# Moving layout transfers to GpSimd and one half of the early recurrences into the projection, in a hybrid gMLP, DeltaNet and attention block

## The chip, the cores and the metric

One core of one Trainium2 chip. The metric is the device time of one execution in microseconds; lower is better. TensorE is called PE below (PEld is its weight load), VectorE DVE, ScalarE ACT, GpSimd POOL and SyncE SP.

## The reference

One sequence of 1024 positions with 2048 channels, in float32. What is computed:

```python
h = rmsnorm(x, ln_g)
proj = h @ w_in
(g_u, g_v, g_z, d_q, d_k, d_v, d_z, d_a, d_b, c_q, c_z) = jnp.split(proj, SPLIT_POINTS, axis=-1)
out_a = gmlp_spatial_gating(g_u, g_v, ...) * silu(g_z)            # 4 groups of 128
q, k, v = split(causal_conv_silu(concat([d_q, d_k, d_v]), conv_w))  # 8 heads of 128
q, k = l2norm(q) * 128 ** -0.5, l2norm(k)
o = gated_delta_rule(q, k, v, g, beta)                           # chunks, state carried along the sequence
out_b = rmsnorm(o, dn_norm_g) * silu(d_z)
out_c = attention(c_q, rmsnorm(mem) @ w_mem_kv) * silu(c_z)      # 256 memory tokens, 4 heads of 128
y = rmsnorm(x + concat([out_a, out_b, out_c]) @ w_out, final_g)
```

In the gated delta rule every chunk needs the inverse of a unit lower triangular matrix `a + eye`, with `a` made from k, beta and the decays; after that a state of 128 x 128 for each head is carried from chunk to chunk.

## The kernel before

The sequence is worked on in two halves of 512 positions (`hf` 0 and 1). Every large product is done as three products of float32r parts: a value is split into `hi` (a cast on ACT, `split_to`) and `lo` (a subtraction on DVE).

The order in which the program is written is not the order in which it is issued. Each call (`S` is ACT, `V` DVE, `G` POOL, `PE` TensorE, `Q` SP) goes to `Plan.add`, which records what it reads and writes. `Plan.price` gives every operation an estimated cost, and for a transfer the time until it has landed. `Plan.issue` then plays the program through with these estimates, on each engine always taking the ready operation of the lowest rank (`rank(...)`, 5 where nothing is said; matmuls of the projection have 9), and issues the operations in the order of their estimated starts. From then on each engine keeps its order: an operation that has to wait holds back all that stand behind it on its engine. Nearly all transfers are issued by SP (`Q.dma_start`).

The stages, in the order of the program:

- Keys and values of the memory, and the normalised rows of x in transposed form (`ahi`, `alo` hold the first half; the second half goes to DRAM as `hTd`).
- The early projection, for heads 0 to 3 alone (pairs p = 0 and 1): `project` computes a column of 128 channels from weight pieces of 4 x 128 rows (four buffers `wraw`). `front(p, hf)` does q and k of a pair: `conv`, then `qk` with the decay mask (POOL's `affine_select` on `E`), the matrices of the chunks into `gt`, and everything stored to DRAM (`late_d`, `gt_d`). `early_values` does v. All this first for half 0; then `refill` loads half 1 into `ahi` and `alo`, and it is done again.
- `blocks_out` writes the diagonal 32 x 32 blocks of `gt` to DRAM (`gdr`, four transfers for a pair and half). `inverse` gathers them into one tile with a block on each partition (`G.dma_start`, `inv<-gdr`), inverts all of them with 62 instructions on DVE, and stores the inverses and their transposes (`tdr`, `udr`). For the early heads it runs once, with the four `gdr` of both halves, on 128 partitions, at rank 3. It uses the two buffers of `inv`, which `qk` needs too.
- The rest of the input projection, five column blocks (`blocks(0)` to `blocks(4)`), each by seven products for two halves of x and two column groups (`seven`), with sums of operands made before (`left_sums`).
- The recurrences. For a pair and half `front_late` loads what was stored, `levels` gathers the inverted blocks (`blocks_in`) and composes the full inverse `ut`, and `back` runs four scan steps and writes the heads' output. For heads 0 to 3 they are written ahead of `blocks(0)` at rank 2.6, and run beside it:

```python
    def backs(ps, inv):
        for hf in range(2):
            for p in ps:
                state = front_late(p, hf, inv[hf * 2 + p % 2])
                ut = levels(state[2], *state[-1])
                if p >= NJ // 2:
                    values(*state)
                back(*state, ut)
```

- Heads 4 to 7 (pairs 2 and 3): their fronts after `blocks(0)`, their inverse ("late") after `blocks(1)`, their recurrences after `blocks(2)`.
- The output projection, seven products for each of two column pairs, and the final norm.

Of the kernel before, what the change touches and what calls it, by code (L numbers as in the profile page):

```python
# [44 lines left out]


class Op:
    __slots__ = ("eng", "fn", "args", "kw", "cls", "idx", "cost", "lat", "nbytes", "lock", "n", "succ", "ready", "at",
                 "lead", "tail", "table")


# [9 lines left out]
class Plan:  # L61
    SEEN = {"pe": 55.0, "act": 35.0, "dve": 35.0, "pool": 78.0, "sp": 60.0}
    SLACK = 600.0
    OVERLAP = {"pe": 0.0, "act": 90.0, "dve": 80.0, "pool": 50.0, "sp": 0.0}
    DMA_RATE = 300.0
    DMA_FIXED = 1600.0
    SWITCH = 250.0
    TABLES = {AF.Exp: "exp", AF.Silu: "silu", AF.Gelu_apprx_tanh: "gelu"}
    TABLE_LOAD = 1500.0
# [113 lines left out]
    def price(self, o, name, outs, ins):  # L183

        out = outs[0]
        n = math.prod(out.shape[1:])
        both = [*outs, *ins]
        psum = any(i.space == PSUM for i in both)
        pointer = any(i.shape[-1] == 1 and math.prod(i.shape[1:]) == 1 for i in ins[1:])
        o.nbytes = o.lock = 0  # L190
        o.lat = 0.0
        if name == "dma_start":
            o.cost = {"sp": 380.0, "act": 430.0, "pool": 1000.0}[o.eng]
            rows = math.prod(out.shape[:-1])
            o.nbytes = max(4 * math.prod(out.shape), 512 * rows)
            src = ins[0]
            pieces = src.shape[-1] < 128 or out.shape[-1] < 128
            if out.space == DRAM:
                o.lat = 9000.0 if out.shape == (32, 8, 32) else 3000.0
            elif pieces or out.shape[0] < 32:  # L200
                o.lat = 2400.0
            elif list(src.ap)[0][0] == 0:
                o.lat = 4000.0
        elif o.eng == "pe":
            passes = 1 if ins[0].dtype == F32R else 2 if name == "transpose" else 4
            o.cost = max(13.3 + n / 2.4 * passes, 222.0 if passes == 4 else 110.0) if out.shape[0] == P else 30.0
            o.lat = 175.0
        elif o.eng == "act":
            o.cost = (165.0 if psum else 200.0) + 0.82 * n + (105.0 if pointer else 0.0)
            o.cost += 190.0 if "accum_out" in o.kw else 0.0  # L210
        elif o.eng == "dve":
            n = max([n] + [math.prod(i.shape[1:]) for i in ins])
            o.cost = (n + 151) / 0.96 + (60.0 if pointer and name == "scalar_tensor_tensor" else 0.0)
            o.lock = not psum and (name.startswith("tensor_") or name == "scalar_tensor_tensor")
            o.lock = o.lock and name != "tensor_reduce"
        else:
            o.lock = 1
            if name in ("memset", "affine_select"):
                o.cost = 100.0 + 0.83 * n * (1 if name == "memset" else 1.4)
                o.lat = 800.0 if name == "affine_select" else 0.0  # L220
            else:
                o.cost = 750.0 + 150.0 * (n - 1) if n < 8 else 200.0 + 2.1 * n

    def issue(self):
# [10 lines left out]
        while left:  # L235
# [22 lines left out]
            for o in (head, *head.tail):  # L258
                t = max(t, free[e])
                if o.table not in (None, table):  # L260
                    t, table = t + self.TABLE_LOAD, o.table
                o.at = t
                left -= 1
                if o.lock:
                    t = max(t, held["pool" if e == "dve" else "dve"])
                end = t + o.cost
                if o.lock:
                    held[e] = end
                free[e] = end - min(self.OVERLAP[e], 0.5 * o.cost)
                done = end + o.lat  # L270
                if o.nbytes and e == "act":
                    beside = max(beside, end) + 2 * o.nbytes / self.DMA_RATE
                    done = beside + self.DMA_FIXED + o.lat
                elif o.nbytes:
                    dma = max(dma, end) + o.nbytes / self.DMA_RATE
                    done = dma + self.DMA_FIXED + o.lat
                for s in o.succ:
                    if s.eng != e or o.nbytes:
# [17 lines left out]
def kernel(  # L296
# [35 lines left out]
    def DT(shape, name, dt=F32):  # L332
        return dr.tile(list(shape), dt, name=name, tag=name)[:]
# [382 lines left out]
    NJ = NH // 2  # L716
# [241 lines left out]
    def blocks_out(gt, n):  # L958

        gv = gt.rearrange("p h t i -> p (h t) i")  # L960
        gdr = [DT([8, 32, 32], f"gdr{n}_{b}") for b in range(4)]
        for b in range(4):
            sl = slice(b * 32, (b + 1) * 32)
            with rank(1):
                S.dma_start(gdr[b].rearrange("c j i -> j c i"), gv[sl, :, sl])
        return gdr

    def flat(start, *aps):
# [2 lines left out]
    def inverse(gdrs, n, cls):  # L971
# [13 lines left out]
        with rank(cls):  # L985
# [240 lines left out]
    def halves(t):  # L1226
# [208 lines left out]
        project_pair(c, lambda hf, b, t, y: dones[b](hf, t, y), dest)  # L1435


    def backs(ps, inv):
        for hf in range(2):
            for p in ps:  # L1440
                state = front_late(p, hf, inv[hf * 2 + p % 2])
                ut = levels(state[2], *state[-1])
                if p >= NJ // 2:
                    values(*state)
                back(*state, ut)
# [93 lines left out]


    with rank(2.6):
        backs(range(NJ // 2, NJ), late_inv)


    def both(c, j, hf, t, y):
# [226 lines left out]
```

## Time and profile before

| | us |
|---|---|
| median of 3 runs | 1661.45 |
| lowest and highest run | 1657.06, 1662.36 |
| the profiled execution, its own time | 1662.46 |
| its span, from first to last instruction | 1660.7 |
| mean granted clock of TensorE | 0.992 |

The profile's times count from the start of the span. "L292" is the line in `Plan.issue` through which every operation is issued, so groups are told apart by the tiles that they write and read: `out<-in`, with the numbers of buffers left out. ACTq, POOLq and SPq are those engines' instruction queues, where transfers are issued. In a list of waits stand the time in total, how often, and the longest; in an order of time the start, the length, the instruction, its count, and in brackets the idle time ahead of it and what ended it. In a list of transfers stand the count, the KB of each and the median time from issue to landing.

### The profile page before, as it was taken

How to read it: one execution, taken by the hardware profiler on the slowest of the kernel's cores; microseconds unless marked ns; L12 is line 12 of the kernel's file. 1: busy time of each engine (PE TensorE's matmuls, PEld its weight loads, DVE VectorE, ACT ScalarE, POOL GpSimd, SP SyncE). 2: the span in 40 equal slices, each digit the busy share in tenths (PEclk: the TensorE clock that was granted, in tenths of full speed). 3: DMA queues.
4: the chain of work that ended last, by engine and by line, in shares of the span. 5: the costliest groups of instructions: out<-in, count | busy, mean ns of one | idle time of the engine just before them, and what ended most of it. 6: DMA issues, size and time to landing. Idle time of an engine off the chain costs nothing.

```text
span 1660.7 us, 26037 instructions
## 1 busy us (share of the span) xinstructions
PE 1623.1 (98%) x8570; PEld 1357.9 (82%) x8570; DVE 1253.7 (75%) x2081; ACT 1027.4 (62%) x2226; POOL 109.2 (7%) x166
## 2 busy tenths in 40 slices
PE   8999999999899999999999998999999999999997
PEld 7888888887788888878887886888888878788886
DVE  4865777778666567989998885777768887688875
ACT  5957765765275556987775345776666774345445
POOL 0000100130000000100013000000000000000001
PEclk9999999999999999999999999999999999999999
DMA  7887888797888886599878977788968769679746
GB/s 253 241 235 222 256 288 244 231 311 269 280 270 263 283 273 201 192 283 337 294 250 274 303 230 205 232 263 305 312 209 291 264 220 353 202 251 307 227 140 241
DMA packets 320625, 427.88 MB, mean 258 GB/s; under 512 B 58669, under 2 KB 139238, under 8 KB 320490
## 3 DMA queue, kind: packets, MB, share of 16 engines
q1 hardware_dynamic: 308290, 418.87, 77.6%
q10 hardware_dynamic: 10088, 4.21, 1.0%
q0 software_dynamic: 2112, 3.15, 0.7%
q8 instruction: 67, 1.10, 0.3%
q14 instruction: 68, 0.56, 0.1%
HBM read 338.52 MB, written 87.06 MB: 256 GB/s over the span
## 4 chain that ended last, share of the span: by engine, by line
PE 82%; DMA 7%; DVE 5%; ACT 2%; issue 2%; SPq 0%; ACTq 0%; DVEq 0%; POOLq 0%; POOL 0%
PE acc L292 62%; PE dn L292 21%; DMA wraw<-in_w_in_dram 2%; DVE wlo L292 1%; DMA wraw<-hTd 1%; DMA wraw<-in_w_out_dram 1%; DVE alo L292 1%; ACT whi L292 1%; DMA y<-in_w_in_dram 1%; DVE y L292 0%; SPq L292 0%; ACTq L292 0%; DMA hTd<-tn 0%; ACT ahi L292 0%; DVE wraw L292 0%
## 5 line engine op out<-in xcount | busy, mean ns | idle before, releaser
L292 PE MATMUL acc<-ahi,whi 128*128 128x512 f32 (+1 forms) x1152 | 451.0, 392 | 1.2 <-ACT whi L292 0.9
L292 PE MATMUL acc<-alo,whi 128*128 128x512 f32 (+1 forms) x1152 | 451.0, 392 | 0.0
L292 PE MATMUL acc<-ahi,wlo 128*128 128x512 f32 (+1 forms) x1152 | 450.3, 391 | 0.2 <-DVE wlo L292 0.2
L292 PEld LDWEIGHTS acc<-ahi,whi 128*128 128x128 f32 x1152 | 217.3, 189 | 43.4 <-ACT whi L292 1.3
L292 PEld LDWEIGHTS acc<-ahi,wlo 128*128 128x128 f32 x1152 | 217.2, 189 | 41.5 <-DVE wlo L292 0.8
L292 PEld LDWEIGHTS acc<-alo,whi 128*128 128x128 f32 x1152 | 217.1, 188 | 40.7
L292 PE MATMUL acc<-ahi,zh 128*128 128x512 f32 x736 | 237.1, 399 | 6.0 <-DVE y L292 5.0
L292 DVE TENSOR_TENSOR wlo<-wraw,whi 128x512 fp32r<-128x512 f32 (+1 forms) x170 | 157.3, 926 | 73.9 <-ACT whi L292 64.5
L292 ACT CAST whi<-wraw 128x512 fp32r<-128x512 f32 (+1 forms) x170 | 137.3, 808 | 121.8 <-PE acc L292 69.1
L292 DVE TENSOR_TENSOR alo<-raws,ahi 128x1024 fp32r<-128x1024 f32 x131 | 159.7, 1220 | 51.0 <-ACT ahi L292 48.3
L292 ACT CAST ahi<-raws 128x1024 fp32r<-128x1024 f32 x131 | 137.4, 1049 | 62.2 <-PE dn L292 28.2
L292 PEld LDWEIGHTS acc<-ahi,zh 128*128 128x128 f32 x736 | 138.7, 191 | 33.9 <-ACT whi L292 5.4
L292 PE MATMUL acc<-ahi,zl 128*128 128x512 f32 x368 | 146.3, 397 | 0.0
L292 DVE TENSOR_TENSOR ahi<-y,ahi 128x1024 fp32r<-128x1024 f32 x65 | 79.2, 1218 | 34.6 <-ACT ahi L292 24.2
L292 ACT CAST ahi<-y 128x1024 fp32r<-128x1024 f32 x65 | 68.1, 1048 | 45.2 <-PE acc L292 20.3
L292 PEld LDWEIGHTS acc<-ahi,zl 128*128 128x128 f32 x368 | 70.1, 190 | 13.7
L292 ACT CAST zh<-wraw 128x1024 fp32r<-128x1024 f32 x36 | 37.8, 1050 | 42.2 <-PE acc L292 25.2
L292 DVE TENSOR_TENSOR zl<-wraw,zh 128x1024 fp32r<-128x1024 f32 x36 | 43.9, 1220 | 21.5 <-ACT zh L292 21.3
L292 PE MATMUL dn<-wlo,ahi 128*128 128x512 f32 x152 | 59.0, 389 | 0.0
L292 PE MATMUL dn<-whi,alo 128*128 128x512 f32 x152 | 59.0, 389 | 0.0
L292 PE MATMUL dn<-whi,ahi 128*128 128x512 f32 x152 | 58.8, 389 | 0.0
L292 POOL TENSOR_TENSOR small<-small,mhalf 128x1 f32<-128x1 f32 x26 | 17.1, 662 | 627.7 <-DVE small L292 627.7
(387 smaller groups left out, 3105.0 us busy)
## 6 DMA issues: line engine op xcount, KB each, us to landing
wraw<-in_w_in_dram SPq DMA_DIRECT2D x268, 256.0 KB, 4.4
raws<-sd SPq DMA_DIRECT2D x148, 256.0 KB, 4.0
y<-in_w_in_dram SPq DMA_DIRECT2D x92, 256.0 KB, 4.7
y<-sd SPq DMA_DIRECT2D x77, 256.0 KB, 4.7
wraw<-in_w_out_dram SPq DMA_DIRECT2D x64, 256.0 KB, 4.1
raws<-h0d SPq DMA_DIRECT2D x54, 256.0 KB, 5.1
y<-in_w_out_dram SPq DMA_DIRECT2D x33, 256.0 KB, 4.1
sd<-zg SPq DMA_DIRECT2D x32, 256.0 KB, 5.9
```

What stands on the lines that cost most here:

```text
L292: o.fn(*o.args, **o.kw)
```

## The change

It does four things.

- The transfers of `blocks_out` (32 in all) go from ACT's queue to POOL's. So do the stores of `inverse`, which become two for each inverse (`tdr`, `udr` over all its partitions) in place of two for each 32 partitions.
- The estimates in `Plan.price` for transfers: the time on the transfer engines is computed from packets (8.5 ns and 0.0368 ns for each byte of a packet, over 16 queues) in place of 300 bytes for each ns; the fixed part is 2900 in place of 1600 ns; issue costs and additional latencies are changed.
- The early inverse is done in two: "early0" with the two `gdr` of half 0, written after the values of half 0, and "early1" with those of half 1, both at rank 5.5.
- The recurrences of pairs 0 and 1 in half 0 are written (rank 2.6) into the projection of half 1, each after the front of the same pair in half 1. Those of half 1 stay ahead of `blocks(0)`. The clearing of the `ut` buffers is written earlier, and `early_values` of half 1 takes PSUM bank 2 or 3 of `dn` for its transposes in place of an `acc` bank.

```diff
@@ class Plan
-    DMA_RATE = 300.0
-    DMA_FIXED = 1600.0
+    PACKET = (8.5, 0.0368)
+    QUEUES = 16
+    DMA_FIXED = 2900.0
@@ def price
-            o.cost = {"sp": 380.0, "act": 430.0, "pool": 1000.0}[o.eng]
-            rows = math.prod(out.shape[:-1])
-            o.nbytes = max(4 * math.prod(out.shape), 512 * rows)
+            o.cost = {"sp": 440.0, "act": 430.0, "pool": 700.0}[o.eng]
             src = ins[0]
-            pieces = src.shape[-1] < 128 or out.shape[-1] < 128
+            run = 4 * min(out.shape[-1], src.shape[-1])
+            fixed, byte = self.PACKET
+            o.moves = 4 * math.prod(out.shape) / run * (fixed + byte * run) / self.QUEUES
             if out.space == DRAM:
-                o.lat = 9000.0 if out.shape == (32, 8, 32) else 3000.0
-            elif pieces or out.shape[0] < 32:
-                o.lat = 2400.0
+                o.lat = 3000.0 if run < 512 else 1500.0
             elif list(src.ap)[0][0] == 0:
-                o.lat = 4000.0
+                o.lat = 3500.0
@@ def issue
-                elif o.nbytes:
-                    dma = max(dma, end) + o.nbytes / self.DMA_RATE
+                elif o.moves:
+                    dma = max(dma, end) + o.moves
                     done = dma + self.DMA_FIXED + o.lat
...
@@ def blocks_out
-                S.dma_start(gdr[b].rearrange("c j i -> j c i"), gv[sl, :, sl])
+                G.dma_start(gdr[b].rearrange("c j i -> j c i"), gv[sl, :, sl])
@@ def inverse
-        tdr, udr = ([DT([32, 32, 32], f"{t}{n}_{i}") for i in range(len(gdrs))] for t in ("tdr", "udr"))
-        for i in range(len(gdrs)):
-            with rank(1):
-                flat(S.dma_start, tdr[i], ti[i * 32 : (i + 1) * 32])
-                flat(S.dma_start, udr[i], gd[i * 32 : (i + 1) * 32])
-        return list(zip(tdr, udr))
+        tdr, udr = (DT([nr, 32, 32], f"{t}{n}") for t in ("tdr", "udr"))
+        with rank(1):
+            flat(G.dma_start, tdr, ti)
+            flat(G.dma_start, udr, gd)
+        return [(tdr[i : i + 32], udr[i : i + 32]) for i in range(0, nr, 32)]
@@ def early_values
-        by_token(vs, to_tokens((v, tpb()))[0], late_hs[:, hf, h, 1])
+        by_token(vs, to_tokens((v, work() if hf else tpb()))[0], late_hs[:, hf, h, 1])
@@ the early projection
     for h in range(NJ):
         early_values(h, 0)
+    with rank(2.6):
+        early_inv = inverse(gdrs, "early0", 5.5)
+
+    def one_back(p, hf, inv):
+        state = front_late(p, hf, inv)
+        ut = levels(state[2], *inv)
+        if p >= NJ // 2:
+            values(*state)
+        back(*state, ut)
...
     first = project([column(0, 0), column(1, 0)], before)
     decays(1, a)
-    gdrs += [front(0, 1, first), front(1, 1)]
-    with rank(3):
-        early_inv = inverse(gdrs, "early", 3)
+    for u in ring["ut"].bufs:
+        G.memset(u, 0.0)
+    gdrs = []
+    for p in range(2):
+        gdrs.append(front(p, 1, first if p == 0 else (None, None)))
+        with rank(2.6):
+            one_back(p, 0, early_inv[p])
+    with rank(2.6):
+        early_inv = inverse(gdrs, "early1", 5.5)
     for h in range(NJ):
         early_values(h, 1)
-    for u in ring["ut"].bufs:
-        G.memset(u, 0.0)
@@ ahead of blocks(0)
     with rank(2.6):
-        backs(range(NJ // 2), early_inv)
+        for p in range(NJ // 2):
+            one_back(p, 1, early_inv[p])
     blocks(0, to_conv(0), to_conv(1))
@@ after blocks(2)
     with rank(2.6):
-        backs(range(NJ // 2, NJ), late_inv)
+        for n, inv in enumerate(late_inv):
+            one_back(NJ // 2 + n % 2, n // 2, inv)
```

More of the change, by code (lines that the diff above doesn't have):

```diff
@@ L47 @@
 class Op:
-    __slots__ = ("eng", "fn", "args", "kw", "cls", "idx", "cost", "lat", "nbytes", "lock", "n", "succ", "ready", "at",
+    __slots__ = ("eng", "fn", "args", "kw", "cls", "idx", "cost", "lat", "moves", "lock", "n", "succ", "ready", "at",
                  "lead", "tail", "table")
@@ L189, in price @@
         pointer = any(i.shape[-1] == 1 and math.prod(i.shape[1:]) == 1 for i in ins[1:])
-        o.nbytes = o.lock = 0
+        o.moves = o.lock = 0
         o.lat = 0.0
         if name == "dma_start":
-            o.cost = {"sp": 380.0, "act": 430.0, "pool": 1000.0}[o.eng]
-            rows = math.prod(out.shape[:-1])
-            o.nbytes = max(4 * math.prod(out.shape), 512 * rows)
+            o.cost = {"sp": 440.0, "act": 430.0, "pool": 700.0}[o.eng]
             src = ins[0]
-            pieces = src.shape[-1] < 128 or out.shape[-1] < 128
+            run = 4 * min(out.shape[-1], src.shape[-1])
+            fixed, byte = self.PACKET
+            o.moves = 4 * math.prod(out.shape) / run * (fixed + byte * run) / self.QUEUES
             if out.space == DRAM:
-                o.lat = 9000.0 if out.shape == (32, 8, 32) else 3000.0
-            elif pieces or out.shape[0] < 32:
-                o.lat = 2400.0
+                o.lat = 3000.0 if run < 512 else 1500.0
             elif list(src.ap)[0][0] == 0:
-                o.lat = 4000.0
+                o.lat = 3500.0
         elif o.eng == "pe":
@@ L270, in issue @@
                 done = end + o.lat
-                if o.nbytes and e == "act":
-                    beside = max(beside, end) + 2 * o.nbytes / self.DMA_RATE
+                if o.moves and e == "act":
+                    beside = max(beside, end) + 2 * o.moves
                     done = beside + self.DMA_FIXED + o.lat
-                elif o.nbytes:
-                    dma = max(dma, end) + o.nbytes / self.DMA_RATE
+                elif o.moves:
+                    dma = max(dma, end) + o.moves
                     done = dma + self.DMA_FIXED + o.lat
                 for s in o.succ:
-                    if s.eng != e or o.nbytes:
+                    if s.eng != e or o.moves:
                         when = done + self.SEEN[s.eng] + (self.SLACK if s.eng == "pe" else 0.0)
@@ L1435, in blocks @@
         project_pair(c, lambda hf, b, t, y: dones[b](hf, t, y), dest)
[L1438 to L1445, printed above, removed]
     with rank(2.6):
-        backs(range(NJ // 2), early_inv)
+        for p in range(NJ // 2):
+            one_back(p, 1, early_inv[p])
     blocks(0, to_conv(0), to_conv(1))
```

## The prediction

> **What bounds the kernel now.** I read the page first, then a table of busy time by stage, then the waits of TensorE (PE), then ScalarE's (ACT's) instructions around the two worst stages.
>
> ```profile
> PE 1623.1 (98%) x8570; PEld 1357.9 (82%) x8570; DVE 1253.7 (75%) x2081; ACT 1027.4 (62%) x2226; POOL 109.2 (7%) x166
> ```
> ```profile
> 0.00:100.00 100.00, 91.28 (x543) 78.48 (x543) 62.69 (x106) 68.19 (x135) 6.37 (x18) 0.97 0.83 256
> 100.00:430.00 330.00, 327.64 (x1570) 271.43 (x1571) 248.57 (x504) 213.53 (x570) 30.85 (x45) 1.00 0.83 260
> 430.00:450.00 20.00, 15.04 (x55) 11.88 (x54) 11.27 (x15) 5.04 (x5) 0.00 (x0) 0.83 0.68 208
> 450.00:1000.00 550.00, 546.18 (x2992) 458.24 (x2991) 435.36 (x714) 356.15 (x763) 53.57 (x74) 1.00 0.81 267
> 1000.00:1020.00 20.00, 13.16 (x110) 10.21 (x110) 13.94 (x20) 8.93 (x15) 1.34 (x3) 0.83 0.75 195
> 1020.00:1630.00 610.00, 607.41 (x3229) 509.41 (x3218) 463.95 (x690) 356.86 (x706) 12.25 (x18) 1.00 0.76 251
> 1630.00:1661.00 31.00, 22.36 (x99) 18.20 (x97) 17.94 (x34) 18.73 (x34) 4.81 (x8) 0.91 0.74 271
> ```
>
> The columns of the table: the stretch, its length, busy time of PE, weight loads, DVE, ACT and POOL (in us), granted clock, DMA share, GB/s. PE nearly always has work, so an edit pays only where it removes idle time or slow clock of PE. Away from the beginning and the end there are two such places. 430 to 450 has 4.96 us of idle and, at clock 0.83, 20 x 0.17 = 3.4 us of lost clock: 8.4 us. 1000 to 1020 has 6.84 and 3.4: 10.2 us. The three long stages between them leave 2.36 + 3.82 + 2.59 = 8.8 us idle together.
>
> ```profile
> PE dn L292 <- DVE el L292: 6.8, 1, 6.8
> PE acc L292 <- DVE y L292: 5.0, 1, 5.0
> ```
> ```profile
> 425.95 1.71 ACTq L292 DMA_DIRECT2D tdrearly<-inv  x3
> 428.78 5.05 ACTq L292 DMA_DIRECT2D udrearly<-inv  x3
> 435.37 0.31 ACTq L292 DMA_DIRECT2D tdrearly<-inv  x1
> 436.09 0.31 ACTq L292 DMA_DIRECT2D udrearly<-inv  x1
> 436.50 1.04 ACT L292 CAST ahi<-y 128x1024 fp32r<-128x1024 f32 x1 [10.15 <-DMA udrearly<-inv]
> ```
> ```profile
> 437.57 1.22 DVE L292 TENSOR_TENSOR ahi<-y,ahi 128x1024 fp32r<-128x1024 f32 x1 [7.56 <-ACT ahi L292]
> ```
> ```profile
> 989.05 3.73 ACTq L292 DMA_DIRECT2D tdrlate<-inv  x4
> 995.51 6.34 ACTq L292 DMA_DIRECT2D udrlate<-inv  x4
> 1001.95 0.62 ACT L292 CAST whi<-kT 128x512 fp32r<-128x512 f32 x1 [12.15 <-DMA tblk<-tdrlate]
> ```
>
> The waits show one wait of PE for each place, both put down to DVE. ACT's order of time shows what stood behind DVE: the eight stores of an inverse (tdr, udr) sit in ACT's own queue, drawn out over 10 and 12 us although a single issue takes 0.31, and the casts of the next operands stand behind them. `ahi` comes 10.15 us late, DVE waits 7.56 for it, and PE runs dry. At 989 it happens again with `whi`.
>
> **The change, part by part.** *The stores of the inverses leave ACT.* Two GpSimd (POOL) transfers for each of three inverses replace sixteen on ACT, so the casts wait for nothing but their data. I count both places as gone: 8.4 + 10.2 = 18.6 us. That is also the most that can be had there. From below: where a load or DVE's own work is next, part of each stays; half is the value I take for that case, 9.3.
>
> *The 32 transfers out of `gt` leave ACT too.*
>
> ```profile
> L292 ACTq DMA_DIRECT2D gdr<-gt x32: 309/469/2578, 187.2 to 888.9; - x32
> gdr<-gt ACTq DMA_DIRECT2D x32, 32.0 KB, 5.1
> inv<-gdr POOLq DMA_DIRECT2D x32, 32.0 KB, 5.4
> L292 POOL DMA_DIRECT2D inv<-gdr x32 | 16.9, 533 | 39.1 <-DMA raws<-sd 18.1 <-DVE hs L292 16.4 <-DMA inv<-gdr 3.3
> L292 POOL DMA_DIRECT2D gt<-kvd x2 | 1.5, 745 | 13.2 <-issue 13.2
> ```
>
> ACT loses 32 x 0.469 = 15 us of issue; PE waits for none of it in the list above, so I count nothing. POOL gets 32 + 6 issues at 0.53 to 0.75 us, 20 to 28 us on an engine busy for 109. Landing is about the same in the rows (5.4 against 5.1). Behind a POOL transfer that waits for an inverse stand the mask of the next head's decay (`affine_select` on E), the rsqrt of `hs` and the clears of `ut` and `gt`; ACT's exponential waits for the mask, and weight casts stand behind that. Between nothing and the 10 to 12 us that ACT lost; I take nothing, since POOL is idle in nine tenths of its time.
>
> The Trainium skill speaks against this part: SBUF — State Buffer, section "SBUF: two separate sides", says that a DMA issued from GpSimd can't write its descriptors while DVE runs a two-port operation such as an fp32 copy within SBUF, with an issue of 620 ns becoming 3100. By that figure the 38 issues would hold POOL for 38 x 3.1 = 118 us, an estimate, and rival 2 below would be the likeliest. The trace does not bear it out for this mix of DVE work: the 32 issues average 533 ns.
>
> *One inverse becomes two.* DVE pays by elements per partition; half as many heads only halve the partitions.
>
> ```profile
> 377.00:427.00 50.00, 0.00 (x0) 0.00 (x0) 22.20 (x63) 0.00 (x0) 0.00 (x0) 1.00 0.83 285
> 298.85 0.64 POOL L292 TENSOR_SCALAR_AFFINE_SELECT E<-E 128x512 f32<-128x512 f32 x1 [83.10 <-ACT vs L292]
> ```
>
> The first row is the time of the instructions on `inv` alone: 63 of DVE, 22.2 us. So DVE gets 22.2 us more. The second row shows the room: POOL has been idle for 83.1 us, since the last `hs` of the first half's heads, when the first mask of the second half comes at 298.85, and in between nobody wants the two `inv` buffers. Should the inverse, at the low rank 5.5, last beyond 299, the second half's heads wait for `inv`, and PE still has the other columns to project.
>
> *The first half's recurrences of two pairs move from the block after into the projection.*
>
> ```profile
> 230.00:300.00 70.00, 69.77 (x324) 57.16 (x323) 51.38 (x103) 40.20 (x95) 0.64 (x1) 1.00 0.83 254
> 300.00:380.00 80.00, 79.95 (x386) 66.75 (x385) 58.19 (x123) 55.81 (x172) 18.43 (x26) 1.00 0.92 282
> 380.00:430.00 50.00, 49.09 (x220) 40.15 (x219) 48.02 (x88) 24.70 (x35) 0.20 (x2) 1.00 0.85 294
> 460.00:660.00 200.00, 198.92 (x1285) 169.89 (x1285) 131.47 (x204) 122.86 (x290) 11.31 (x18) 1.00 0.78 255
> ```
> ```profile
> 439.00:660.00 221.00, 28.84 (x176) 26.03 (x176) 8.59 (x28) 7.51 (x32) 0.98 0.78 251
> 439.00:660.00 221.00, 19.29 (x112) 17.04 (x112) 8.72 (x28) 0.00 (x0) 0.98 0.78 251
> 439.00:660.00 221.00, 4.40 (x32) 3.84 (x32) 8.59 (x28) 32.04 (x130) 0.98 0.78 251
> ```
> ```profile
> L292 SPq DMA_DIRECT2D kT<-late x8: 320/348/454, 337.7 to 597.6; - x8
> ```
> ```profile
> kT<-late SPq DMA_DIRECT2D x16, 256.0 KB, 4.3
> gt<-gtd SPq DMA_DIRECT2D x8, 512.0 KB, 4.8
> ```
> ```profile
> 1521.80 43.52 PE acc L292 x192
> ```
>
> PE's work only changes its place: 0. The three rows of 439 to 660 are the instructions on `steps`, `states` and `vs` while four recurrences ran: DVE (8.59 + 8.72) / 4 = 4.3 us for one, ACT (7.51 + 32.04) / 4 = 9.9, and some 4 of copies in `levels`. From 230 to 380 DVE has 18.6 + 21.8 = 40.4 us free and gets 22.2 + 2 x 4.3 = 30.8; ACT has 54.0 free and gets 28. Both fit. DMA is tighter. A recurrence loads ten tiles of 256 KB and one of 512, gathers the inverse's blocks (0.3 MB) and stores two tiles, 4.0 MB in all, which at 282 / 0.92 = 307 GB/s fills the engines for 13 us. Two are 26, of which the first one's loads (3.1 MB, 10 us) run before 430 already (`kT<-late` begins at 337.7): 16 us more. Free are 11.9 + 6.4 + 7.5 = 25.8 us over the three rows. Each load is also one more place in SP's queue ahead of a weight load, at rank 2.6 against 4; four weight pieces are buffered, of 12 matmuls at 43.52 / 192 = 0.227 us each, so 10.9 us of cover against a burst of 10. Bounds: 0, and 16 + 10 - 6.4 = 19.6 us when all 26 falls on the fullest row, 300 to 380. I take 4 us, nearest to the last of the four rows, where recurrences ran at a DMA share of 0.78 and PE lost 1.1 us in 200, and more than that because this stage is fuller. What the following block gains by losing two of its four recurrences is at most that 1.1.
>
> *The new estimates* (a transfer's time by its packets, 2.9 us fixed for 1.6) reorder every queue. The rows above say loads land after 4 to 5 us, so the order should fit better; the 8.8 us of small idle time may shrink or double. I take 0.
>
> **Sum.** The profiled execution took 1662.5 us (span 1660.7), 1.0 above the median of 1661.45. 1662.5 - 18.6 + 4 = 1647.9, or 1647 against the median.
>
> **Rivals.** *1, slower: the projection starves.* The two bursts of loads and the second inverse fall where DMA is at 0.92 and DVE between 0.73 and 0.96. If all 19.6 us becomes idle time of PE, and the clock falls with it as at 1000 (10.2 lost for 6.84 idle, a factor 1.5), it costs 29: 1662.5 - 18.6 + 29 - 1 = 1672. It turns to a loss from 12.4 us of idle on. For it: no DMA row is as full as 300 to 380. Against it: PE was idle there for 0.05 us.
>
> ```profile
> 430.00:440.00 10.00, 6.32 (x28) 4.88 (x26) 2.44 (x4) 2.56 (x3) 0.00 (x0) 1.00 0.88 304
> 440.00:450.00 10.00, 8.72 (x27) 7.00 (x28) 8.82 (x12) 2.48 (x3) 0.00 (x0) 0.66 0.48 111
> ```
>
> One idle piece of 5 us was followed by a clock of 0.66 in the next ten. The Trainium skill (TensorE: Matmul & The Clock Gate, Part 1) puts the threshold at an idle window of about 3.4 us: if the 19.6 came in shorter pieces the clock would hold, and this rival would give 1662 instead of 1672, an estimate.
>
> *2, POOL inherits the queue.* Masks wait behind the stores, ACT behind the masks, and half of the gain stays: 1662.5 - 9.3 - 1 = 1652. For it: ACT's stores were drawn out to 10 us. Against it: POOL's idle share.
>
> *3, the new order costs what the stores gave.* Small waits all over triple, 8.8 to 27: 1661. Against it: the latencies in the estimates come nearer to the rows.
>
> **Chances.** Forecast 0.60, rival 1 0.18, rival 2 0.12, rival 3 0.10. About 0.3% (5 us) is what a measurement of this kernel can tell from no change. Faster takes the forecast less its upper tail and nearly all of rival 2: 0.68. Same takes rival 3 and those tails: 0.12. Slower: 0.20. The range goes down to 1635, where also the 4 us and most of the 8.8 us go, and up to 1669, which leaves out the upper half of rival 1.
>
> **What would show it.** Right: no ACT wait of 10 us behind tdr or udr; no clock of 0.83 around the first product block and the late recurrences; DVE about 22 us busier, PE's count about 8570; `steps` and `states` busy from about 310 on. Wrong: PE waits for `whi` or `wlo` between 300 and 430, or an ACT wait for E behind a POOL transfer.

## The result, and the profile after

The kernel after takes 1662.4 us (median of 15 runs, 1657.85 to 1667.35), the kernel before 1661.38 (15 runs, 1657.06 to 1666.81) beside it: ratio 1.0003, 95% interval 0.9991 to 1.0015. No change, where 1647 was forecast. The profiled execution of after took 1665.71 us (span 1663.9), 3.3 above its median.

The page's line of busy time, and the table by stage of the kernel after (columns as in the prediction; the line of `Plan.issue` is L291 now):

```profile
PE 1625.6 (98%) x8570; PEld 1359.5 (82%) x8570; DVE 1272.1 (76%) x2144; ACT 1034.1 (62%) x2228; POOL 137.1 (8%) x206
```
```profile
0.00:100.00 100.00, 92.30 (x558) 78.63 (x559) 64.84 (x117) 71.05 (x144) 6.89 (x18) 1.00 0.86 263
100.00:430.00 330.00, 324.52 (x1779) 271.33 (x1778) 243.46 (x538) 224.27 (x643) 53.46 (x75) 0.99 0.84 256
430.00:450.00 20.00, 20.00 (x97) 16.78 (x96) 18.83 (x36) 14.25 (x25) 0.00 (x0) 1.00 0.93 308
450.00:1000.00 550.00, 536.90 (x2885) 447.79 (x2884) 444.50 (x727) 349.96 (x730) 62.92 (x92) 0.99 0.81 264
1000.00:1020.00 20.00, 17.46 (x170) 14.51 (x169) 16.20 (x24) 13.94 (x37) 1.36 (x3) 0.91 0.70 228
1020.00:1630.00 610.00, 610.00 (x2984) 510.62 (x2984) 464.27 (x673) 340.88 (x617) 7.64 (x10) 1.00 0.76 250
```

The stop at 430 to 450 is gone, 20.00 busy at clock 1.00. Of that at 1000 to 1020, 2.54 us of idle and, reckoned as in the prediction, 20 x 0.09 = 1.8 of lost clock are left, 4.3 for 10.2. So 14.3 of the 18.6 us came, where they were expected. They went again in the two long stages that had been full: 100 to 430 is now idle for 5.48 us (2.36 before), 450 to 1000 for 13.1 (3.82 before). From 100 to 1630 PE is idle for 21.1 us, and before for 20.6.

Where, in the same columns, in the kernel after:

```profile
320.00:340.00 20.00, 15.61 (x85) 13.23 (x85) 8.03 (x17) 11.26 (x35) 1.50 (x2) 0.85 1.01 299
490.00:510.00 20.00, 15.48 (x147) 12.62 (x146) 11.84 (x15) 9.48 (x20) 0.61 (x2) 0.95 0.68 200
720.00:750.00 30.00, 27.39 (x131) 22.41 (x130) 26.69 (x45) 26.34 (x64) 0.63 (x1) 1.00 0.81 281
890.00:910.00 20.00, 17.61 (x100) 14.10 (x99) 15.55 (x26) 9.02 (x13) 6.45 (x9) 0.83 0.96 302
950.00:970.00 20.00, 17.06 (x183) 14.35 (x182) 10.83 (x20) 12.89 (x34) 0.82 (x3) 1.00 0.94 331
```

Five places hold 4.39 + 4.52 + 2.61 + 2.39 + 2.94 = 16.9 us of idle and some 6 of lost clock. PE's waits in the kernel after name what was late (a wait of 4.4 us for `y`, in the first 100 us, is left out between the first two lines):

```profile
PE dn L291 <- ACT vs L291: 8.8, 3, 4.4
PE dn L291 <- DMA tblk<-tdrearly: 2.4, 1, 2.4
PE dn L291 <- DMA tblk<-tdrlate: 2.4, 2, 1.8
PE dn L291 <- DMA ut<-udrearly: 2.0, 1, 2.0
PE dn L291 <- DVE ai L291: 1.5, 2, 1.3
PE dn L291 <- DVE inv L291: 1.3, 1, 1.3
```

All write `dn`, and none is the projection's `acc` (its longest wait from 100 us on is 0.4): they are matmuls of the recurrences, of `levels` and of the fronts, placed in PE's queue ahead of what they read. 6.8 us are the gathers of the inverted blocks (`tblk`, `ut`). The wait for `vs` at 335 is a chain through three queues; the orders of time of SP, DVE, ACT and PE in the kernel after:

```profile
324.27 1.07 SPq L291 DMA_DIRECT2D zg<-hTd  x2
```
```profile
332.63 0.69 DVE L291 TENSOR_TENSOR zg<-zg 128x512 f32<-128x512 f32 x1 [5.39 <-DMA zg<-hTd]
```
```profile
334.76 0.27 ACT L291 COPY vs<-dn 128x128 f32<-128x128 f32 x1 [6.18 <-DVE states L291]
```
```profile
335.08 1.48 PE L291 MATMUL dn<-states,kT 128*128 128x128 f32 x4 [4.39 <-ACT vs L291]
```

A load for the left sums (`zg`) lands 7 to 8 us after its issue, in a stretch with a DMA share of 1.01. Behind the sum that waits for it DVE holds the copies of `states`; ACT holds `vs` for those, PE the scan step for `vs`.

### The profile page after: what moved, and what is told of

Its sections match the earlier page's. It is cut to its first block, busy times and chain, and to the rows that moved or that the text cites. A ratio compares the mean times of both kernels' runs of the same rounds, so it can differ in the third digit from the quotient of the medians.

```text
span 1663.9 us, 26164 instructions
## 1 busy us (share of the span) xinstructions
PE 1625.6 (98%) x8570; PEld 1359.5 (82%) x8570; DVE 1272.1 (76%) x2144; ACT 1034.1 (62%) x2228; POOL 137.1 (8%) x206
## 4 chain that ended last, share of the span: by engine, by line
PE 77%; DMA 10%; DVE 6%; issue 4%; ACT 2%; SPq 1%; POOLq 0%; POOL 0%; DVEq 0%; ACTq 0%
PE acc L291 57%; PE dn L291 20%; DMA wraw<-in_w_in_dram 3%; DVE wlo L291 1%; SPq L291 1%; DMA y<-sd 1%; DMA zg<-hTd 1%; DMA y<-in_w_in_dram 1%; DVE alo L291 1%; DMA xr<-pd 1%; ACT ahi L291 1%; DVE y L291 1%; DMA kT<-in_mem_dram 1%; DVE kT L291 1%; ACT whi L291 0%
## 5 line engine op out<-in xcount | busy, mean ns | idle before, releaser
L291 PE MATMUL acc<-ahi,wlo 128*128 128x512 f32 (+1 forms) x1152 | 451.6, 392 | 0.3 <-DVE wlo L291 0.3
L291 PE MATMUL acc<-alo,whi 128*128 128x512 f32 (+1 forms) x1152 | 451.6, 392 | 0.0
L291 PE MATMUL acc<-ahi,whi 128*128 128x512 f32 (+1 forms) x1152 | 451.2, 392 | 0.0
L291 PEld LDWEIGHTS acc<-ahi,wlo 128*128 128x128 f32 x1152 | 217.4, 189 | 41.5 <-DVE wlo L291 0.7
L291 PEld LDWEIGHTS acc<-ahi,whi 128*128 128x128 f32 x1152 | 217.4, 189 | 41.5 <-ACT ahi L291 0.2
L291 PEld LDWEIGHTS acc<-alo,whi 128*128 128x128 f32 x1152 | 217.4, 189 | 40.9
L291 PE MATMUL acc<-ahi,zh 128*128 128x512 f32 x736 | 235.1, 398 | 0.0
L291 DVE TENSOR_TENSOR wlo<-wraw,whi 128x512 fp32r<-128x512 f32 (+1 forms) x170 | 156.9, 924 | 66.9 <-ACT whi L291 63.5
L291 ACT CAST whi<-wraw 128x512 fp32r<-128x512 f32 (+1 forms) x170 | 137.0, 808 | 109.4 <-PE acc L291 67.0
L291 DVE TENSOR_TENSOR alo<-raws,ahi 128x1024 fp32r<-128x1024 f32 x131 | 159.9, 1220 | 38.3 <-ACT ahi L291 37.9
L291 ACT CAST ahi<-raws 128x1024 fp32r<-128x1024 f32 x131 | 137.4, 1049 | 68.6 <-PE dn L291 28.1
L291 PEld LDWEIGHTS acc<-ahi,zh 128*128 128x128 f32 x736 | 137.5, 190 | 26.7
L291 PE MATMUL acc<-ahi,zl 128*128 128x512 f32 x368 | 145.8, 396 | 0.3 <-DVE zl L291 0.3
L291 DVE TENSOR_TENSOR ahi<-y,ahi 128x1024 fp32r<-128x1024 f32 x65 | 79.3, 1221 | 22.2 <-ACT ahi L291 22.1
L291 ACT CAST ahi<-y 128x1024 fp32r<-128x1024 f32 x65 | 68.2, 1049 | 33.8 <-PE acc L291 12.3
L291 PEld LDWEIGHTS acc<-ahi,zl 128*128 128x128 f32 x368 | 69.9, 190 | 14.6 <-DVE zl L291 0.7
L291 POOL TENSOR_TENSOR small<-small,mhalf 128x1 f32<-128x1 f32 x26 | 17.3, 670 | 662.6 <-DVE small L291 662.6
L291 PE MATMUL dn<-wlo,ahi 128*128 128x512 f32 x152 | 59.0, 389 | 0.0
L291 PE MATMUL dn<-whi,alo 128*128 128x512 f32 x152 | 59.0, 389 | 0.0
L291 PE MATMUL dn<-whi,ahi 128*128 128x512 f32 x152 | 58.8, 389 | 0.0
L291 ACT CAST zh<-wraw 128x1024 fp32r<-128x1024 f32 x36 | 37.8, 1050 | 33.1 <-PE acc L291 20.8
L291 POOL TENSOR_TENSOR hs<-hs,mhalf 128x4 f32<-128x4 f32 x32 | 43.4, 1357 | 177.7 <-DVE hs L291 177.5
```

What stands on the lines that cost most here:

```text
L291: o.fn(*o.args, **o.kw)
```

## The experiments

The change has four parts, and each theory gives one of them the loss. Theory 1: the new estimates place matmuls ahead of their data. Theory 2: the recurrences in the projection cost it. Theory 3: any new order of this program idles some 20 us somewhere. All kernels are timed in five rounds beside the kernel before, which had 1661.4 to 1662.6 us in these sessions; a ratio is to it, with its 95% interval.

### The parts alone and in pairs

`e_transfers` has only the first part of the change, `e_estimates` only the new estimates, `e_trans_est` both, `e_trans_moved` everything but the new estimates; `e_moved` and `e_est_moved` are the kernel before and the kernel with new estimates, with recurrences and inverses as after and the transfers on ACT.

> The kernel before with the transfers alone moved to POOL (the 32 out of gt, the stores of the inverses), old estimates, recurrences where they were. Theory 1 (the new estimates of the small gathers place the matmuls of `levels` ahead of their data; the stores gave what was predicted): both old stalls are gone and nothing new comes, 1643 to 1650. Theory 2 (the recurrences in the projection cost it): the same, 1643 to 1650. Theory 3 (any new order leaves about 20 us of idle time in the middle, whatever is moved): 1655 to 1665.

> The kernel before with the new estimates alone; stores on ACT, recurrences where they were. Theory 1: the two old stalls stay and the waits of PE for tblk and ut come on top, 1666 to 1674. Theory 2: as before, 1658 to 1665. Theory 3: anywhere within 1655 to 1668.

> Transfers on POOL and the new estimates, recurrences where they were. Theory 1: still waits of PE for tblk and ut, 1655 to 1664. Theory 2: the gain of the stores is there, 1643 to 1651. Theory 3: 1655 to 1665.

> Transfers on POOL and the recurrences moved, with the old estimates. Theory 1: no waits of PE for tblk or ut, 1643 to 1651. Theory 2: a stall of PE in the projection of the second half, 1655 to 1664. Theory 3: 1655 to 1665.

> The kernel before with the recurrences of half 0 moved and the inverse in two, transfers on ACT, old estimates. Theory 2 (recurrences in the projection cost about 8 us): 1669, with new waits of PE between 250 and 430. If moving them helps as it did with the transfers on POOL (28.6 us less): 1635 to 1650. Theory 3: 1655 to 1690 whatever is moved.

> The kernel after with the stores of the inverses and the transfers out of gt back on ACT. If the stores' price of 18.6 us adds up with the rest: 1662.4 + 18.6 = 1681, with ACT waits of 10 us behind tdr or udr around 300, 440 and 890. Theory 3 (the losses are those of an order, and don't add up): anything from 1655 to 1690.

| transfers | estimates | recurrences | kernel | median, us | ratio |
|---|---|---|---|---|---|
| ACT | old | old place | before | 1661.4 | 1 |
| ACT | old | moved | e_moved | 1666.62 | 1.0025 [1.0015, 1.0035] |
| ACT | new | old place | e_estimates | 1679.21 | 1.0098 [1.0081, 1.0115] |
| ACT | new | moved | e_est_moved | 1670.23 | 1.0047 [1.0031, 1.0064] |
| POOL | old | old place | e_transfers | 1686.64 | 1.0142 [1.0122, 1.0163] |
| POOL | old | moved | e_trans_moved | 1658.04 | 0.9975 [0.9963, 0.9988] |
| POOL | new | old place | e_trans_est | 1654.32 | 0.995 [0.9932, 0.9968] |
| POOL | new | moved | after | 1662.4 | 1.0003 [0.9991, 1.0015] |

The parts don't add up. The transfers' move is worth, down the pairs, +25.2, -8.6, -24.9 and -7.8 us; the recurrences' move +5.2, -9.0, -28.6 and +8.1. The new estimates are worth +17.8, +3.6, -32.3 and +4.4. A price for a part alone, such as theory 2's, does not exist here.

`e_trans_moved` goes against theory 1, which had 1643 to 1651 without the new estimates: it takes 1658.04, though no wait of PE for a gather is left. PE idles in other places in it, 9.0 us from 100 to 430 (2.76 of them for `alo`, an operand of the projection) and 7.3 from 450 to 1000:

```profile
100.00:430.00 330.00, 321.01 (x1764) 267.66 (x1763) 242.09 (x535) 221.43 (x642) 48.10 (x73) 0.99 0.81 249
```

That is what theory 2 expected of this kernel, and theory 3 too. `e_estimates` lies above what every theory had for it (1674 at most). The largest surprise is `e_transfers`, which no theory had above 1665. Its worst stage:

```profile
1210.00:1290.00 80.00, 60.01 (x359) 48.72 (x358) 35.63 (x69) 37.81 (x118) 3.89 (x6) 0.79 0.57 181
```
```profile
1068.48 0.58 POOL L292 DMA_DIRECT2D tdrlate<-inv  x1 [91.00 <-issue]
```
```profile
1271.84 0.80 PE L292 MATMUL dn<-steps,ut 128*128 128x128 f32 x2 [6.13 <-DVE steps L292]
```

Its first 1020 us go as forecast: from 1000 to 1020 PE is busy for all 20.00 us. But the late inverse is stored at 1068 (before: 989 to 1002), and the late recurrences end at 1288 (before: 1225). They reach further into the stage in which the blocks end and attention and gating are finished; there PE waits again and again for the scan's operands, 20 us idle, and a clock of 0.79. The late fronts, which feed this inverse, store their blocks at 754 to 965 (before: 715 to 887). Why they come so much later in this order I read from no trace and did not try.

### The line that the new estimates dropped

Old estimates had 2400 ns more for loads of small pieces, and the change drops it. By `Plan.price` a gather of the inverted blocks (128 to 256 packets of 128 bytes) is now due 2900 + 106 to 211 ns = 3.0 to 3.1 us after its issue, and a load `inv<-gdr` (8 packets of 4 KB) after 2900 + 80 = 3.0. Before the change they were due after 1600 + 2400 + 218 to 437 = 4.2 to 4.4 us, and after 4.1. What they take in the kernel after, from its list of transfers:

```profile
tblk<-tdrearly SPq DMA_DIRECT2D x20, 16.0 KB, 4.5
tblk<-tdrlate SPq DMA_DIRECT2D x20, 16.0 KB, 4.9
ut<-udrearly SPq DMA_DIRECT2D x16, 32.0 KB, 1.9
ut<-udrlate SPq DMA_DIRECT2D x16, 32.0 KB, 3.8
inv<-gdr POOLq DMA_DIRECT2D x32, 32.0 KB, 5.8
```

So in the median the new estimates are 1.5 and 1.9 us short for the gathers of `tblk` and 2.8 short for `inv<-gdr`; for the gathers of `ut` they are not, or by less than one. How long a gather takes hangs on the order too: in the kernel before the same lines have 2.8, 2.5, 2.5 and 2.7, for which 3.0 would have done in the median, and only `inv<-gdr`, with 5.4, stood far from it.

`e_after_lat` puts the line back in the kernel after. As the fixed part stays at 2900, these loads are then due after some 5.4 us, later than with the old estimates:

```diff
             if out.space == DRAM:
                 o.lat = 3000.0 if run < 512 else 1500.0
+            elif run < 512 or out.shape[0] < 32:
+                o.lat = 2400.0
```

> The kernel after with one line of the old estimates put back: 2400 ns more for loads of small pieces (the gathers tblk, ut, raws). Theory 1 (the new estimates put the matmuls of levels ahead of their data): the PE waits for tblk and ut (2.4 + 2.4 + 2.0 us, and the slow clock of 3.1 us around 900) go, 1652 to 1655, and no PE wait for tblk or ut over 0.5 us is left. Theory 2 (the recurrences in the projection are the cost): those waits may go, but PE's wait for vs and states at 330 (4.4 and 1.7 us) stays, 1656 to 1660. Theory 3 (any new order of this program loses some 17 to 30 us at new places): waits of the same size come up elsewhere, 1655 to 1680.

1650.65 us (1644.7 to 1652.44), ratio 0.9922 [0.9904, 0.994]: 11.7 us less than after, a little more than theory 1 had. The five places in `e_after_lat`:

```profile
320.00:340.00 20.00, 20.00 (x181) 17.43 (x176) 13.90 (x27) 17.41 (x50) 6.67 (x8) 1.00 0.90 276
490.00:510.00 20.00, 19.56 (x234) 16.67 (x234) 11.23 (x17) 12.62 (x34) 0.61 (x2) 1.00 0.69 209
720.00:750.00 30.00, 29.45 (x139) 24.34 (x139) 27.60 (x45) 26.03 (x56) 4.29 (x6) 1.00 0.86 293
890.00:910.00 20.00, 19.71 (x110) 15.87 (x105) 18.96 (x32) 7.93 (x10) 3.46 (x6) 1.00 0.80 251
950.00:970.00 20.00, 18.58 (x152) 16.57 (x153) 14.63 (x26) 13.43 (x35) 0.20 (x1) 0.91 0.96 311
```

In these five 16.9 us of idle became 2.7, and no wait for `tblk` or `ut` over 0.3 us is left. Part of it came back beside them: PE waits 2.20 us at 942 and 1.39 at 973, and of its 2.46 at 951 the last line shows only a part. From 100 to 1630 the idle time falls from 21.1 to 12.2 us. The stop at 330, which was theory 2's, went too, though no recurrence was moved back.

Two kinds of load that matter here share the line. `e_after_gather` and `e_after_inv` put it back for one of them each:

```diff
+            elif run == 128 and o.eng == "sp":               # e_after_gather: tblk, ut
+            elif o.eng == "pool" and out.shape[0] < 32:      # e_after_inv: inv<-gdr
+                o.lat = 2400.0
```

> The kernel after with the old 2400 ns put back for the gathers of the inverted blocks alone (tblk, ut; not for the other small loads). Theory 1: it is these, so 1648 to 1654, as with all small loads (1650.65). Theory 3: 1655 to 1670.

> The kernel after with the 2400 ns put back for the loads inv<-gdr on GpSimd alone. Theory 1 with both kinds at fault: these bring what the gathers did not, 11.7 - 5.7 = 6.0 us, so 1655 to 1658, with the PE waits for tblk and ut left (some 5 us) and the wait for vs at 330 gone. If the gathers alone are at fault: 1661 to 1664. Theory 3 (accident of the order): 1655 to 1670 with waits at other places.

1656.71 us (0.9969 [0.9957, 0.9982]) and 1652.22 (0.9946 [0.9928, 0.9964]): 5.7 and 10.2 us. Either helps, the loads of the inverse more than theory 1 had, the gathers less; together they give 11.7, not the sum. In `e_after_inv` PE still waits 7.2 us for `tblk`, more than the kernel after does, and it is the faster by 10.2: the waits for the gathers that theory 1 named are not what most of the gain is made of. What the second one does is seen on POOL, first in the kernel after, then in `e_after_inv`:

```profile
291.16 0.70 POOL L291 DMA_DIRECT2D tdrearly<-inv  x1 [66.52 <-DVE inv L291]
...
295.64 0.64 POOL L291 TENSOR_SCALAR_AFFINE_SELECT E<-E 128x512 f32<-128x512 f32 x1 [3.04 <-ACT vs L291]
```
```profile
296.23 1.90 POOL L293 TENSOR_SCALAR_AFFINE_SELECT E<-E 128x512 f32<-128x512 f32 x2 [71.71 <-ACT vs L293]
300.88 0.71 POOL L293 DMA_DIRECT2D tdrearly<-inv  x1 [2.76 <-DVE inv L293]
```

With the inverse due later the masks of the second half come first, and the recurrence's first matmul with `tblk` at 319.7 in place of 314.6. PE then has no wait from 318 to 340. In `e_after_gather`, where the store stays ahead of the masks (293.96) and that matmul comes at 317.4, the stop stays:

```profile
335.08 0.69 DVE L293 TENSOR_TENSOR zg<-zg 128x512 f32<-128x512 f32 x1 [5.29 <-DMA zg<-hTd]
```

That the order of store and masks decides it is not shown: in `e_lat_slack`, below, the store (299.51) is ahead of the masks (300.26) too, that matmul comes at 319.3, and PE has no wait from 300 to 345.

### How much an accidental order is worth

`e_control` (on after) and `e_lat_control` (on `e_after_lat`) alter an estimate that the change doesn't touch. `e_lat_slack` places every matmul later behind its operands, `e_lat_both` does both.

```diff
-    SLACK = 600.0
+    SLACK = 1000.0                                          # e_lat_slack, e_lat_both
-    OVERLAP = {"pe": 0.0, "act": 90.0, "dve": 80.0, ...
+    OVERLAP = {"pe": 0.0, "act": 90.0, "dve": 85.0, ...     # the controls, e_lat_both
```

> The kernel after with one estimate altered that has nothing to do with the change: the overlap of neighbouring DVE instructions 85 in place of 80 ns. The order of all engines changes in places. Theory 1: the losses lie where the gathers' estimate is too short, so they come back: 1659 to 1666, with PE waits for tblk or ut of some 5 us in all. Theory 3 (the losses are those of an accidental order): a time that differs from 1662.4 by over 5 us, and other waits.

> The kernel after with the 2400 ns for all small loads put back, and the overlap of DVE instructions 85 in place of 80 ns, an estimate that has nothing to do with it. Theory 1: 1648 to 1654. Theory 3: away from 1650.65 by over 5 us, back to about 1660.

> The kernel after with the 2400 ns put back and every matmul placed 400 ns later behind its operands (slack 1000 in place of 600 ns). If what is left in the middle of the program (12 us idle) is matmuls placed too close behind their data: 1643 to 1648. If a later order only shifts the wait to the engines behind PE: 1650 to 1660.

> The kernel after with the 2400 ns put back, slack 1000 in place of 600 ns and DVE overlap 85 in place of 80 ns: the two alterations that gave 1649.0 and 1646.9 each. If their gains were of the order's making and add up by half: 1643 to 1647. If they are the scatter of orders: 1645 to 1655.

| | without the line | with it |
|---|---|---|
| as it is | 1662.4, 1.0003 | 1650.65, 0.9922 [0.9904, 0.994] |
| overlap 85 | 1664.72, 1.002 [1.0009, 1.0031] | 1646.91, 0.991 [0.9891, 0.993] |
| slack 1000 | | 1649.04, 0.9923 [0.9906, 0.994] |
| both | | 1654.74, 0.9964 [0.9951, 0.9977] |

The overlap alone shifts the time by 2.3 and 3.7 us here, by 5.7 on top of the slack, and by 5.4 with the recurrences in their old place (`e_te_lat_control` below, where theory 3's "over 5 us" came true): the scatter of an order is 2 to 6 us. Two alterations that helped alone are together worse than either. With the line there are 1647 to 1655 us, without it 1662 and 1665, 7.7 apart at the least: theory 3 is right about the scatter, and too small for the difference in the kernel after. `e_control` shows both sides: its total stays where theory 1 has it, but not with the waits that it named (`tblk` 3.8 us, and 7.1 for `inv` where there were 1.3); its profiled execution took 1673.94 us, 9.2 above the median, so these waits may be larger than usual. `e_lat_control` is the fastest kernel of the study, 0.9% under before; from 100 to 1630 PE idles for 6.6 us in its profiled execution, which took 4.2 us less than the median. Which of the four with the line is best is scatter, and says nothing about slack or overlap.

### What the other parts are worth with the line put back

`e_est_moved_lat` is `e_after_lat` with the transfers back on ACT. `e_trans_est_lat` and `e_te_lat_control` have the transfers on POOL and the recurrences in their old place, `e_two_inv` and `e_two_inv_lat` the inverse in two besides (without and with the line):

```diff
     for h in range(NJ):
         early_values(h, 0)
+    with rank(2.6):
+        early_inv = inverse(gdrs, "early0", 5.5)
...
-    gdrs += [front(0, 1, first), front(1, 1)]
-    with rank(3):
-        early_inv = inverse(gdrs, "early", 3)
+    gdrs = [front(0, 1, first), front(1, 1)]
+    with rank(2.6):
+        early_inv = early_inv + inverse(gdrs, "early1", 5.5)
```

> The kernel after with the same line put back, and the stores of the inverses and the transfers out of gt back on ACT. It prices the transfers' move in a mended order: 1650.65 + 18.6 = 1669 if my price of the stores holds there, 1650.65 + 7.8 = 1658 if it is what the unmended order showed (1670.2 against 1662.4).

> Transfers and new estimates, recurrences in their old place, with the 2400 ns for loads of small pieces put back. Theory 1: its PE waits for ut, tblk and el (2.0, 1.7 and 1.7 us, and about 1 us of clock) go: 1647 to 1650. If the recurrences' new place only paid once the order is mended, this stays near 1654 while the kernel after with the same line has 1650.65. Theory 3: 1652 to 1670.

> The same two lines in the kernel with the recurrences in their old place (1650.33 without the second). Theory 1: 1648 to 1654; and the recurrences' new place is worth less than 3 us either way. Theory 3: away by over 5 us.

> Transfers and new estimates, with the early inverse done in two (early0, early1, rank 5.5) as in the kernel after, but the recurrences of half 0 left in the block after. It parts the second inverse from the moved recurrences. Theory 2: the second inverse costs nothing (DVE has 40 us free from 230 to 380), so 1652 to 1657, as without the split (1654); the 8 us that the kernel after loses against it come from the recurrences. Theory 1: the same. Rival: the inverses on DVE hold back the casts at 300 to 430, about 1662. Theory 3: 1655 to 1680.

> Transfers, new estimates with the 2400 ns for small loads put back, the early inverse in two, recurrences of half 0 in their old place. If the recurrences' move clears the stop at 450: PE still stops there for 5 to 8 us, 1650 to 1656. If the second inverse does: no stop over 3 us at 440 to 470, 1644 to 1649.

| kernel | median, us | ratio |
|---|---|---|
| e_est_moved_lat | 1665.82 | 1.0026 [1.0014, 1.0038] |
| e_trans_est_lat | 1650.33 | 0.9935 [0.992, 0.9951] |
| e_te_lat_control | 1655.71 | 0.9964 [0.9953, 0.9976] |
| e_two_inv | 1660.43 | 0.998 [0.9968, 0.9992] |
| e_two_inv_lat | 1654.24 | 0.9961 [0.9946, 0.9975] |

*The transfers.* 1665.82 - 1650.65 = 15.2 us, nearer to my 18.6 than to the 7.8 without the line. ACT's queue in `e_est_moved_lat` shows the old picture at one of the three inverses, stores drawn out and an operand behind them, and a stop of PE of 3.5 us:

```profile
903.48 4.67 ACTq L293 DMA_DIRECT2D tdrlate<-inv  x4
908.20 0.60 ACT L293 ACTIVATE steps<-dn 128x512 f32<-128x512 f32 x1 [6.21 <-DMA tdrlate<-inv]
```
```profile
908.85 0.66 PE L293 MATMUL dn<-ident,ut 128*128 128x128 f32 x4 [3.48 <-ACT steps L293]
```

The rest of the 15.2 us I did not trace to the stores.

*The recurrences.* In their old place with the line there are three kernels of 1650.3, 1654.2 and 1655.7 us, moved four of 1646.9 to 1654.7: a gain of some 3 us in the means, inside the scatter. Pair by pair the move with the inverse's split gains -0.3 and 8.8 us (the second pair with overlap 85), the move alone 3.6. Their old place has a stop of its own, in `e_trans_est_lat` at 450. SP, DVE, ACT and PE:

```profile
432.47 3.06 SPq L293 DMA_DIRECT2D tblk<-tdrearly  x5
436.03 2.26 SPq L293 DMA_DIRECT2D ut<-udrearly  x4
438.34 0.45 SPq L293 DMA_DIRECT2D tblk<-tdrearly  x1
438.83 3.83 SPq L293 DMA_DIRECT2D ut<-udrearly  x8
442.76 2.97 SPq L293 DMA_DIRECT2D pd<-y  x4
445.82 1.20 SPq L293 DMA_DIRECT2D y<-in_w_in_dram  x2
```
```profile
450.25 0.69 DVE L293 TENSOR_TENSOR y<-y,y 128x512 f32<-128x512 f32 x1 [11.12 <-DMA y<-in_w_in_dram]
```
```profile
453.84 1.04 ACT L293 CAST zh<-wraw 128x1024 fp32r<-128x1024 f32 x1 [8.12 <-DVE wraw L293]
```
```profile
456.15 1.22 PE L293 MATMUL dn<-vs,ut 128*128 128x128 f32 x4 [7.26 <-ACT ut L293]
```

SP issues 18 gathers and four stores in 13 us ahead of a weight load; the sum of weights on DVE waits for that load, the cast on ACT for the sum, `ut` stands behind the cast, and PE waits for `ut`. `e_te_lat_control` idles for 8.4 us at the same place, `e_after_lat` nothing. In `e_two_inv_lat` PE waits 2.0 us there, so inverses at other times clear most of it without the move; but as the total came to 1654.24 and not 1644 to 1649, clearing it did not pay by itself. `e_two_inv` without the line has 1660.43: the split without the move already has most of the 8.1 us between 1654.3 and 1662.4 that I had put down to the recurrences.

*The line.* In the kernel after it is worth 11.7 us, and 17.8 with overlap 85. In the three other pairs that differ by it alone it is worth less: 4.0 with the recurrences in their old place (1654.32 and 1650.33), 6.2 with the inverse in two besides (1660.43 and 1654.24), 4.4 with the transfers on ACT (1670.23 and 1665.82). These are within the scatter or at its end.

## Why the prediction was wrong

- **The stores, 18.6 us.** Right in mechanism and nearly in size: 14.3 us came at the two places, and no ACT wait behind tdr or udr is left. The term was somewhat too large, as it counted the slow clock over idle time too: over PE's busy time it is 15.04 x 0.17 = 2.6 and 13.16 x 0.17 = 2.2, and both places hold 16.6 us, of which 12.5 came by the same count.
- **The new estimates, 0 us.** This is the step that failed: I took 0 for a new order of every queue. The 8.8 us of small idle time in the three long stages, which "may shrink or double", became 5.48 + 13.1 + 0 = 18.6. I wrote that loads land after 4 to 5 us "so the order should fit better". That holds for the fixed part, raised to 2900, but I didn't work out what the new price gives for the loads that the recurrences and the inverse wait for. The diff shows it: the 2400 ns go, 4.2 us becomes 3.0, and the quoted row of `inv<-gdr` had 5.4. In this kernel the dropped line costs 11.7 us, and the sum with it would be 1659. That is not the same as new against old: with the old estimates and all the rest of the change (`e_trans_moved`) there are 1658.04 us and 16.3 of small idle time, so the new ones as a whole cost 4.4, and 11 us over the forecast would have been there without them. The 0 was my only term for the order itself. What makes the idle time that is there with the old estimates, no experiment here takes apart.
- **The recurrences in the projection, 4 us.** Not shown to cost anything by themselves: with the line put back their place is clean (328.5 of 330 us busy from 100 to 430) and the move is worth -9 to +0.3 us. With the old estimates and the transfers on ACT (`e_moved`) it costs 5.2, within the scatter, with PE idle for 10.2 us from 100 to 430. What I feared of DMA came at one place: the stop at 335, 4.4 us of idle and a clock of 0.85, begins with a late load in a row with a DMA share of 1.01. It goes with the estimate of the inverse's loads (`e_after_inv`), no recurrence moved.
- **One inverse becomes two, 0 us.** The 22 us of DVE are there (the instructions on `inv` take 102.6 us in place of 80.7) and lie beside PE's work with the line (1654.2 against 1650.3 and 1655.7). Without the line the split costs 6.1 us (1660.4 against 1654.3), at the upper end of the scatter.
- **POOL.** 28 us busier, the upper end of what was worked out; ACT waits for it hardly more than before (6.7 us for `hs`, 6.1 before; 0.3 for `E`). No issue is held up:

```profile
L291 POOL DMA_DIRECT2D gdr<-gt x32 | 19.3, 608 | 55.7 <-DVE gt L291 55.5
```

In the kernel after an issue of this group takes 608 ns and one of `inv<-gdr` 519, and the longest of all on POOL 778, with DVE busy for 76% of the span; rival 2 did not come. DVE's copies take only 13 us in all there. The Trainium skill (SBUF — State Buffer, "SBUF: two separate sides") gives some 3100 ns for a GpSimd DMA overlapped by a copy on DVE, and 620 for one alone. I laid that on all 38 issues, though copies are so small a part of DVE's work here; whether it holds for an issue beside a copy these runs do not settle.

- **The rivals.** Rival 3 (1661, the new order gives the gain back) came, in a few stops rather than the "small waits all over" of its text. Rival 1 has little support: the stop at 335 apart, no wait of PE for a weight cast is over 0.3 us.

Open are why the transfers alone delay the late inverse by 69 to 79 us, how the dropped line's 11.7 us divide among the stops, why it is worth only 4 to 6 in the other settings, and what the recurrences' place is worth below a scatter of up to 6 us.

## What to carry to other kernels

Where estimates decide the order on engines that keep it, a change of the estimates is a change of the kernel: work out the new number for each load on which a matmul waits, and hold it against the landing time in the trace, as those that fall short can turn into stops. The trace before is not enough for it, as landing times change with the order (the gathers of `tblk` from 2.5 to 4.9 us here). Price parts in pairs, not alone: here the same move of transfers gave from -25 to +25 us by what stood beside it. And before a difference of a few us is put down to an edit, alter an unrelated estimate and see what the order's scatter is; here it is 2 to 6 us and as large as most of the terms.

## What the hardware showed unexpectedly

Short stops cost clock too. At 898.68 PE waited 0.58 us for `tblk<-tdrlate` and at 900.92 1.81 more, with small matmuls of 32 x 32 between; by 2 us, in the kernel after:

```profile
900.00:902.00 2.00, 1.08 (x27) 1.02 (x28) 1.52 (x3) 0.09 (x1) 1.77 (x2) 0.65 1.32 337
902.00:904.00 2.00, 2.00 (x8) 1.71 (x8) 2.00 (x4) 1.23 (x3) 0.64 (x2) 0.50 1.06 377
904.00:906.00 2.00, 2.00 (x7) 1.51 (x6) 1.28 (x4) 0.00 (x0) 0.00 (x0) 0.50 0.63 160
```

2.4 us of idle in two pieces were followed by a clock of 0.50; in these rows 0.4 + 1.0 + 1.0 us are lost, as much as the stop. One piece alone does it as well: PE stands still for 2.54 us up to 1005.55, with no small matmul on either side, and then:

```profile
1006.00:1008.00 2.00, 2.00 (x8) 1.56 (x7) 1.69 (x4) 1.66 (x5) 0.00 (x0) 0.60 1.04 340
1008.00:1010.00 2.00, 2.00 (x8) 1.38 (x6) 1.24 (x2) 0.55 (x2) 0.00 (x0) 0.54 0.87 324
```

After stops of 1.97 and 1.85 us, at 495 and 956 in the same trace, the clock stays at 1.00. The Trainium skill (TensorE: Matmul & The Clock Gate, Part 1) has the clock fall after an idle window of about 3.4 us; the piece of 2.54 us was shorter, and the measurement decides. My line that shorter pieces would hold the clock does not stand.
